# Units 30 to 67 of the weight stream: the low half of each weight tile on GpSimd instead of VectorE

## The chip, the core and the metric

One Trainium2 chip; the program runs on one of its cores. The metric is device time in microseconds (us) from the first to the last instruction of an execution, plus a small constant. It is measured over three runs; one further execution is recorded by the hardware profiler, and every row below is of that one.

## The reference, cut to what matters

One decoder layer on 512 tokens of width 2048, in float32:

- x1 = x + W_out · concat[conv_group(xn), swa_group(xn)], with xn = RMSNorm(x) and proj = xn @ W_in + b_in. The first 2048 columns of proj feed the convolution group: a GLU (a · sigmoid(gate)), a causal depthwise convolution with 31 taps over 1024 channels, LayerNorm over the channels, swish. The rest are q, k and v of a sliding-window attention with 16 heads of 64.
- y = x1 + PEER(RMSNorm(x1)): product-key retrieval of 16 of 16384 single-neuron experts for each of 8 heads. The kernel computes most tokens densely over all experts and the last tokens by gathered rows.

Matrix products have to come out at float32 precision. The kernel writes each float32 matrix as hi + lo, where hi is the value rounded to the type that TensorE multiplies fast (float32r) and lo is the rest, and sums three products: hi·hi, hi·lo and lo·hi.

## The kernel before, in words

**The weight stream.** All weights come through one stream of 628 units of 128x1024 float32 (512 KB). `stream` (lines 124 to 137) does four things for a unit: SyncE loads it into a raw buffer (line 131; two raw buffers in this part of the kernel), ScalarE rounds it into w_hi (line 135), VectorE subtracts to make w_lo (line 136), and both tiles are kept for TensorE. Of w_hi and of w_lo there are three buffers each. `unit()` asks for one unit more than is being used.

**Which units are which.** Units 0 to 51 are the input projection, thirteen groups of four units: k/v, then query groups and GLU groups in turn, and from unit 32 on only GLU groups (channels 3 to 7). Units 30 and 31 are the second half of the last query group. Units 52 to 67 are the half of the output projection that takes the attention result ("attention half", lines 572 to 590), units 68 to 83 the half that takes the convolution result ("convolution half"). Units 84 to 115 are the PEER queries, all later ones the experts.

**What lies beside the matmuls.** Two hand-made queues of small jobs are emptied a little after every unit by `pump`, by estimated costs: attention steps in the first, the convolution in the second. A GLU group ends with two multiplications from PSUM (lines 498, 499), a sigmoid, a GpSimd memset of the 30 padding columns of a new h tile (line 502; two h buffers, so it waits until the convolution of two groups before has read its h), the gated product into h (line 503), and 31 taps on VectorE (lines 287, 289), each a multiply-add of two 128x512 SBUF tiles. When all 8 channel groups are through, LayerNorm follows: their sum s (lines 455, 457), its mean by a matmul with ones (line 461, lnmu), subtraction (466), squares on ScalarE (472) summed on VectorE (473), the statistics by matmuls (262, 269), then per channel group a multiplication (480), swish (481) and the split into mh and ml (171, 172). The convolution half's first matmul needs mh, its second ml. The LayerNorm jobs are entered behind the attention half's matmuls in the program; the marks `urgent` and `high_priority` move them ahead by 200 instructions in the planner's order.

**What sets the order.** Each engine works through its own queue in a fixed order. The order comes from a planner that runs when the kernel is built: it takes, by its own estimate of the times, the instruction that is ready and stands first in the program, after priorities. The loads, w_hi and w_lo have a priority offset of 400. If an engine's real times differ from the plan, the order stays.

**GpSimd** (POOL in the profile) has, before the gathers of the PEER part begin, constants, two memsets for the v tiles and the eight memsets of h.

Of the kernel before, what the change touches and what calls it, by code (L numbers as in the profile page):

```python
# [9 lines left out]
FT = mybir.dt.float32  # L10
# [4 lines left out]
OP = mybir.AluOpType  # L15
# [12 lines left out]
START = 10  # L28
END = 250.0
PUMP = 5.4  # L30
CONV_K = 31
HD, NQ = 64, 16
NK, PH, TOPK = 128, 8, 16
# [2 lines left out]
C_N1, C_N2, C_CB, C_LG, C_LB, C_BA, C_BG, C_CW = 0, 16, 32, 40, 48, 56, 64, 72  # L36
N_PAR = C_CW + 8 * CONV_K
R_B, R_SK, R_QG, R_KG = 0, 1280, 1296, 1360
# [21 lines left out]
def hymba_layer(ctx: ExitStack, tc: tile.TileContext, xT, pos, par, row, wi, wo, wq, sk, ut, un, vt, vn,  # L60
                out_t, out_r, dbg=None):
    nc = tc.nc
# [18 lines left out]
    def later(cost, fn, *a, low=False):  # L81
        queues[low].append((cost, fn, a))
# [11 lines left out]
    def drain(low=True):  # L94
        for q in queues[:1 + low]:
            while q:
                _, fn, a = q.popleft()
                fn(*a)
# [26 lines left out]
    def stream(upto):  # L125
        while nxt[0] < min(upto, len(specs)):
            i = nxt[0]
            nxt[0] += 1
            raw = raws[-1][0].tile([128, 1024], FT, name="w_raw", bufs=raws[-1][1])
            with tc.high_priority(offset=400 if i >= 4 else 0):  # L130
                nc.sync.dma_start(raw, specs[i])
            hi = ring.tile([128, 1024], FR, name="w_hi", bufs=3)
            lo = ring.tile([128, 1024], FR, name="w_lo", bufs=3)
            with tc.high_priority(offset=400):
                nc.scalar.activation(hi, raw, AF.Copy)  # L135
                nc.vector.tensor_tensor(lo, raw, hi.bitcast(FT), op=OP.subtract)  # L136
            units[i] = (hi, lo)

    def unit(ahead=1):
        i = nxt[1]  # L140
        nxt[1] += 1
        stream(i + 1 + ahead)
        return units.pop(i)
# [19 lines left out]
    def par_col(base, c):  # L163
        return P[:, base + c:base + c + 1]
# [72 lines left out]
    for c in range(KC):  # L237
        if c % 4 == 0:
            stream(c // 4 + 1)
        xr = px.tile([128, T], FT, name="xr", bufs=4)  # L240
        nc.sync.dma_start(xr, xT[c])
        nc.scalar.activation(xh[:, c], xr, AF.Copy, scale=par_col(C_N1, c))
        nc.vector.scalar_tensor_tensor(xl[:, c], xr, par_col(C_N1, c), xh[:, c].bitcast(FT), op0=OP.mult,
                                       op1=OP.subtract)
        if c == 0:
            nc.scalar.activation(ssq, xr, AF.Square)
        else:
            sq = px.tile([128, T], FT, name="sq", bufs=2)
            nc.scalar.activation(sq, xr, AF.Square)
            nc.vector.tensor_tensor(ssq, ssq, sq, op=OP.add)  # L250
# [30 lines left out]
    def conv_chunk(c, h):  # L281
        first = [True]

        def tap(k):
            w = par_col(C_CW, c * CONV_K + k)
            if k == 0:
                nc.vector.tensor_scalar(mix_c[:, c], h[:, :T], w, par_col(C_CB, c), op0=OP.mult, op1=OP.add)
            else:
                nc.vector.scalar_tensor_tensor(mix_c[:, c], h[:, k:k + T], w, mix_c[:, c], op0=OP.mult, op1=OP.add)  # L289
        for k in range(CONV_K):  # L290
            later(0.66, tap, k, low=True)
# [192 lines left out]
    def glu_group(g):  # L484
# [15 lines left out]
        nc.scalar.activation(tg, tg, AF.Sigmoid, bias=par_col(C_BG, g))  # L500
        h = pa_.tile([128, CONV_K - 1 + T], FT, name="h", bufs=2)
        nc.gpsimd.memset(h[:, :CONV_K - 1], 0.0)
        nc.vector.scalar_tensor_tensor(h[:, CONV_K - 1:], ta, par_col(C_BA, g), tg, op0=OP.add, op1=OP.mult)
        conv_chunk(g, h)
# [279 lines left out]
    for h in range(PH):  # L784
# [6 lines left out]
        for u in range(4):  # L791
            hi, lo = unit()
# [123 lines left out]
    def step(first, us):  # L916
        tick[0] += 1
        if tick[0] > START:
            gather_until(int((tick[0] - START) * STEPS / (END - START)) + 1, first)
        pump(us)  # L920
# [18 lines left out]
    for e in range(8 * AHEAD):  # L939
# [3 lines left out]
        if e % 4 == 3:  # L943
            nc.scalar.dma_start(H[e // 4], gl)
        step(first, PUMP)
    drain()
# [149 lines left out]
```

## Time and profile before

| | us |
|---|---|
| median of 3 runs | 2863.24 (2862.2 to 2864.12) |
| the profiled execution | 2863.08 |
| its span, first to last instruction | 2861.3 |
| PE (TensorE) busy | 2811.3 (98%) |
| DVE (VectorE) busy | 2368.2 (83%) |
| ACT (ScalarE) busy | 1214.2 (42%) |
| POOL (GpSimd) busy | 471.7 (16%) |

The span is cut into 40 slices of 71.5 us for the overview of the page; a digit is the busy share of a slice in tenths. The third to the seventh slice hold the stretch of units 30 to 67. Busy times of neighbouring instructions overlap a little: VectorE's 128x1024 subtraction is listed at 1.23 us, and the next one starts 1.14 us after it. TensorE's busy time is modelled from pipelined matmuls, and a full share does not say that it runs at its best clock; the granted clock stands in a column of its own (1.00 is 2.4 GHz).

### The profile page before, as it was taken

To read this page: it belongs to the slowest core of one execution; us is meant where nothing else is said; L and a number is where in the kernel's file an instruction comes from. 1 tells how busy PE (TensorE), PEld (TensorE's weight loads), DVE (VectorE), ACT (ScalarE), POOL (GpSimd) and SP (SyncE) were. 2 spreads that over 40 slices of the span, in tenths; PEclk is the share of its full clock that TensorE was granted. 3 is DMA by queue.
4 is the path that set the end of the run, shared out by engine and by line. 5 is a ranking of instruction groups with operands and counts; after the bars stand their busy time and mean duration, and the time that the engine had idled before them with its cause. 6 is when DMAs were issued, how large, how long until landed. Compare 5 with 4: busy or idle time off the path is not lost. (4 is left out here: it accounts for less than half of the span.)

```text
span 2861.3 us, 43542 instructions
## 1 busy us (share of the span) xinstructions
PE 2811.3 (98%) x16995; PEld 2688.8 (94%) x16995; DVE 2368.2 (83%) x3586; ACT 1214.2 (42%) x1879; POOL 471.7 (16%) x337
## 2 busy tenths in 40 slices
PE   8999999999999999999999999999999999999999
PEld 8998877788899999999999999999999999999999
DVE  7888996569999887777787878878888899997984
ACT  5666434343343787666332333333333333333332
POOL 0000000000002222212212222222222223222320
PEclk9999999999999999999999999999999999999999
DMA  5222332523249999899998989898898999998994
GB/s 174 75 67 74 115 100 85 170 93 136 89 157 345 325 325 339 311 341 339 349 351 321 343 313 359 335 336 336 326 344 323 372 361 350 354 366 329 358 347 147
DMA packets 204207, 764.00 MB, mean 267 GB/s; under 512 B 18593, under 2 KB 70945, under 8 KB 160417
## 3 DMA queue, kind: packets, MB, share of 16 engines
q1 hardware_dynamic: 103584, 378.66, 36.7%
q0 software_dynamic: 46080, 335.56, 31.0%
q10 hardware_dynamic: 54336, 47.00, 5.0%
q8 instruction: 133, 2.18, 0.3%
q14 instruction: 74, 0.60, 0.1%
HBM read 716.42 MB, written 44.70 MB: 266 GB/s over the span
## 5 line engine op out<-in xcount | busy, mean ns | idle before, releaser
L135 ACT ACTIVATE w_hi<-w_raw 128x1024 fp32r<-128x1024 f32 x628 | 666.0, 1061 | 1277.7 <-PE mm L981 536.1
L136 DVE TENSOR_TENSOR w_lo<-w_raw,w_hi 128x1024 fp32r<-128x1024 f32 x628 | 772.1, 1233 | 276.6 <-ACT w_hi L135 275.4
L932 PE MATMUL mm<-nl,w_hi 128*128 128x352 f32 x2048 | 668.2, 326 | 0.0
L930 PE MATMUL mm<-nh,w_hi 128*128 128x352 f32 x2048 | 664.9, 325 | 1.0 <-ACT w_hi L135 1.0
L979 PE MATMUL mm<-ah,w_hi 128*128 128x352 f32 x2048 | 658.4, 323 | 7.4 <-DVE acc L989 7.4
L933 PE MATMUL mm<-nh,w_lo 128*128 128x352 f32 x2048 | 664.0, 325 | 0.0
L981 PE MATMUL mm<-al,w_hi 128*128 128x352 f32 x2048 | 660.3, 323 | 0.0
L982 PE MATMUL mm<-ah,w_lo 128*128 128x352 f32 x2048 | 645.0, 323 | 12.7 <-DVE w_lo L136 12.5
L982 PEld LDWEIGHTS mm<-ah,w_lo 128*128 128x128 f32 x2048 | 380.9, 188 | 18.0 <-DVE w_lo L136 17.9
L979 PEld LDWEIGHTS mm<-ah,w_hi 128*128 128x128 f32 x2048 | 384.0, 188 | 9.2 <-DVE acc L989 7.6
L930 PEld LDWEIGHTS mm<-nh,w_hi 128*128 128x128 f32 x2048 | 385.3, 188 | 1.5 <-ACT w_hi L135 1.3
L933 PEld LDWEIGHTS mm<-nh,w_lo 128*128 128x128 f32 x2048 | 385.4, 188 | 0.1
L932 PEld LDWEIGHTS mm<-nl,w_hi 128*128 128x128 f32 x2048 | 384.8, 188 | 0.1
L981 PEld LDWEIGHTS mm<-al,w_hi 128*128 128x128 f32 x2048 | 384.8, 188 | 0.0
L826 POOL DMA_INDIRECT grow<-un,idx x86 | 121.3, 1411 | 898.9 <-DVE grow L842 591.3
L859 DVE SCALAR_TENSOR_TENSOR yrow<-grow,h,yrow 128x2048 f32<-128x2048 f32 x107 | 251.4, 2349 | 1.5 <-DMA grow<-vn,idxb 1.4
L842 DVE SCALAR_TENSOR_TENSOR grow<-grow,xrow 128x2048 f32<-128x2048 f32 x107 | 244.6, 2286 | 0.8 <-DMA grow<-un,idxb 0.8
L989 DVE TENSOR_TENSOR acc<-acc,mm 128x352 f32<-128x352 f32 x240 | 118.8, 521 | 87.4 <-PE mm L982 87.3
L826 POOL DMA_INDIRECT grow<-vn,idx x85 | 125.4, 1475 | 391.5 <-DVE yrow L859 381.6
L289 DVE SCALAR_TENSOR_TENSOR mix_c<-h,par,mix_c 128x512 f32<-128x512 f32 x240 | 173.8, 750 | 1.6
L859 DVE SCALAR_TENSOR_TENSOR yrow<-xrow,h,yrow 128x2048 f32<-128x2048 f32 x53 | 124.6, 2351 | 0.0
L842 DVE SCALAR_TENSOR_TENSOR yrow<-yrow,xrow 128x2048 f32<-128x2048 f32 x53 | 121.2, 2286 | 2.9 <-DMA xrow<-XB 2.9
(274 smaller groups left out, 3979.3 us busy)
## 6 DMA issues: line engine op xcount, KB each, us to landing
w_raw<-ut SPq DMA_DIRECT2D x256, 512.0 KB
w_raw<-vt SPq DMA_DIRECT2D x256, 512.0 KB
w_raw<-wi SPq DMA_DIRECT2D x52, 512.0 KB
G<-gt ACTq DMA_DIRECT2D x22, 1024.0 KB
Gb<-G SPq DMA_DIRECT2D x16, 1408.0 KB
w_raw<-wo SPq DMA_DIRECT2D x32, 512.0 KB
w_raw<-wq SPq DMA_DIRECT2D x32, 512.0 KB
H<-gl ACTq DMA_DIRECT2D x18, 704.0 KB
```

Source lines behind the costliest of these rows:

```text
L135: nc.scalar.activation(hi, raw, AF.Copy)
L136: nc.vector.tensor_tensor(lo, raw, hi.bitcast(FT), op=OP.subtract)
L289: nc.vector.scalar_tensor_tensor(mix_c[:, c], h[:, k:k + T], w, mix_c[:, c], op0=OP.mult, op1=OP.add)
L826: i = nc.gpsimd.indirect_dma_start(out=g, out_offset=None, in_=src, in_offset=bass.IndirectOffsetOnAxis(ap=at, axis=0))
L842: nc.vector.scalar_tensor_tensor(g, g, 1.0, rows["x"], op0=OP.mult, op1=OP.mult, accum_out=h3[:, k:k + 1])
L859: nc.vector.scalar_tensor_tensor(y, g, h3[:, k:k + 1], y, op0=OP.mult, op1=OP.add)
L930: m = nc.tensor.matmul(bank, hi[:, s], nh[:, k, :TD], start=k == 0, stop=False)
L932: nc.tensor.matmul(bank, hi[:, s], nl[:, k, :TD], start=False, stop=False)
L933: nc.tensor.matmul(bank, lo[:, s], nh[:, k, :TD], start=False, stop=k == KC - 1)
L979: m = nc.tensor.matmul(banks[j], hi[:, ws], ah[:, ee], start=ee == 0, stop=False)
L981: nc.tensor.matmul(banks[j], hi[:, ws], al[:, ee], start=False, stop=False)
L982: nc.tensor.matmul(banks[j], lo[:, ws], ah[:, ee], start=False, stop=ee == 7)
```

## The change

`stream` picks the engine of the subtraction by the unit's number: GpSimd for units 30 to 67, VectorE for all others. The loads, w_hi, buffers, priorities and the order of the program's text stay.

```diff
+POOL_LO = (30, 68)
...
             with tc.high_priority(offset=400):
                 nc.scalar.activation(hi, raw, AF.Copy)
-                nc.vector.tensor_tensor(lo, raw, hi.bitcast(FT), op=OP.subtract)
+                eng = nc.gpsimd if POOL_LO[0] <= i < POOL_LO[1] else nc.vector
+                eng.tensor_tensor(lo, raw, hi.bitcast(FT), op=OP.subtract)
             units[i] = (hi, lo)
```

## Rows read from the trace of the kernel before

**Rows 1.** The page's overview: busy tenths in 40 slices.
```profile
PE   8999999999999999999999999999999999999999
DVE  7888996569999887777787878878888899997984
POOL 0000000000002222212212222222222223222320
```

**Rows 2.** Busy by stretch: window, length; PE, PEld, DVE, ACT, POOL busy; clock, DMA.
```profile
203.00:437.00 234.00, 231.46 (x1202) 195.43 (x1201) 217.37 (x388) 107.89 (x208) 0.50 (x4) 1.00 0.28 93
```

**Rows 3.** VectorE's groups in 203 to 437 us: count | busy us, mean ns | idle before.
```profile
L289 DVE SCALAR_TENSOR_TENSOR mix_c<-h,par,mix_c 128x512 f32<-128x512 f32 x180 | 129.0, 751 | 1.0
L136 DVE TENSOR_TENSOR w_lo<-w_raw,w_hi 128x1024 fp32r<-128x1024 f32 x37 | 45.3, 1225 | 6.3 <-ACT w_hi L135 6.1
L172 DVE TENSOR_TENSOR pl<-ptr,ph 128x512 fp32r<-128x512 f32 x14 | 9.6, 687 | 2.6 <-ACT ph L171 2.6
L398 DVE CUSTOM_DVE_ANT_0 sm<-sc,maskb 128x256 f32<-128x256 f32 x24 | 9.1, 423 | 0.0
...
L498 DVE TENSOR_TENSOR tg<-mm,rstd 128x512 f32<-128x512 f32 x6 | 4.1, 686 | 0.0
```

**Rows 4.** VectorE in order of time, 436 to 467 us: start, length, instruction [idle before].
```profile
436.69 0.68 DVE L457 TENSOR_TENSOR s<-s,mix_c 128x512 f32<-128x512 f32 x1
...
444.05 4.91 DVE L466 TENSOR_TENSOR mix_c<-mix_c,mu 128x512 f32<-128x512 f32 x8 [1.72 <-ACT mu L463]
...
454.25 3.08 DVE L473 TENSOR_TENSOR lnss<-lnss,lnsq 128x512 f32<-128x512 f32 x4
...
462.29 4.87 DVE L480 TENSOR_TENSOR mix_c<-mix_c,stat 128x512 f32<-128x512 f32 x8 [1.25 <-PE stat L269]
```

**Rows 5.** TensorE in order of time, 442 to 466 us.
```profile
442.36 1.02 PE L461 MATMUL lnmu<-s,ones 128*128 128x512 f32 x2
...
457.39 0.40 PE L582 MATMUL mm<-mah,w_lo 128*128 128x512 f32 x1
...
465.10 2.08 PE L580 MATMUL mm<-mh,w_hi 128*128 128x512 f32 x4 [2.86 <-ACT mh L171]
```

**Rows 6.** Busy by stretch behind the attention half, columns as in rows 2.
```profile
460.00:470.00 10.00, 5.42 (x17) 3.93 (x18) 6.86 (x12) 9.30 (x16) 0.00 (x0) 0.61 0.18 54
470.00:480.00 10.00, 10.00 (x39) 7.98 (x39) 4.42 (x6) 4.00 (x7) 0.00 (x0) 0.87 0.00 0
```

**Rows 7.** GpSimd's memsets of large tiles, grouped as in rows 3.
```profile
L855 POOL MEMSET yrow<- 128x2048 f32 x1 | 1.8, 1812 | 10.9 <-DMA out_r<-yrow 10.9
L348 POOL MEMSET vh<- 128x1024 f32 x1 | 1.0, 954 | 40.0 <-PE rowstat L262 40.0
```

**Rows 8.** One GpSimd instruction: duration ns min/median/max.
```profile
L826 POOL DMA_INDIRECT grow<-un,idx x86: 935/1681/2751, 678.0 to 1662.3; - x86
```

**Rows 9.** GpSimd and VectorE in order of time around 928 and 946 us.
```profile
927.88 0.94 POOL L826 DMA_INDIRECT grow<-un,idx  x1 [5.18 <-DVE grow L842]
...
946.33 1.68 POOL L826 DMA_INDIRECT grow<-un,idx  x1 [5.75 <-DVE grow L842]
...
928.73 1.23 DVE L136 TENSOR_TENSOR w_lo<-w_raw,w_hi 128x1024 fp32r<-128x1024 f32 x1 [1.11 <-ACT w_hi L135]
...
945.98 1.22 DVE L136 TENSOR_TENSOR w_lo<-w_raw,w_hi 128x1024 fp32r<-128x1024 f32 x1
```

**Rows 10.** ScalarE's w_hi two units apart, in order of time.
```profile
428.86 1.06 ACT L135 ACTIVATE w_hi<-w_raw 128x1024 fp32r<-128x1024 f32 x1 [4.01 <-PE mm L581]
...
440.01 1.06 ACT L135 ACTIVATE w_hi<-w_raw 128x1024 fp32r<-128x1024 f32 x1 [4.01 <-PE mm L581]
```

**Rows 11.** Who waited for the loads of line 131, 200 to 460 us (us, times).
```profile
  ACT w_hi L135: 1.4, 1
```

**Rows 12.** GpSimd's queue in order of time, 246 to 387 us.
```profile
309.99 0.12 POOL L502 MEMSET h<- 128x30 f32 x1 [63.27 <-DVE mix_c L289]
...
386.60 0.12 POOL L502 MEMSET h<- 128x30 f32 x1 [32.45 <-DVE mix_c L289]
```

## The prediction, made before the result was known

> **What bounds the kernel now.** I read the page's overview first. TensorE's row shows 9 in every slice but the first; VectorE's shows 8 and 9 up to the sixth, and GpSimd's shows 0 until the gathers start [rows 1]. So TensorE bounds the kernel, and a change on other engines can give back only time in which TensorE waits, or add to it. The next view is busy time by stretch: between 203 and 437 us, where units 30 to 66 get their low halves, VectorE is busy 217.4 of 234 us, GpSimd 0.5, ScalarE 107.9, and TensorE is short of the window by 2.5 us [rows 2]. There is little to win inside the stretch.
>
> The loss lies at its end. In TensorE's order of time the attention half's last matmul starts at 457.39 and the convolution half's first at 465.10, after a wait for ScalarE's mh [rows 5]. A matmul of this shape follows the last one after 0.23 us (two units of 24 in 11.15 us [rows 10]), so TensorE lacks 465.10 - 457.62 = 7.5 us. The clock pays again: 0.61 in the ten microseconds of the gap and 0.87 in the next ten, against 1.00 before [rows 6]. From 465.1 to 480 that costs roughly 10 x 0.13 = 1.3 us behind 470 and 5 x 0.5 = 2.4 us ahead of it (half speed while the gap is fresh), 3.7 us in all. The transition is worth 11 us.
>
> What ends last there is LayerNorm. In VectorE's order, the sum s is complete at 436.69 + 0.68 = 437.4; the mean's matmul lnmu runs at 442.36, the subtractions start at 444.05, the last squares are summed by 457.3, the multiplications start at 462.29 [rows 4, 5]. From lnmu to the first mh matmul it is 465.10 - 442.36 = 22.7 us. So the question is when s is complete, and that is VectorE's work: s comes after the last of the taps.
>
> **What the change removes.** 38 subtractions leave VectorE, 37 of them by 437 us: 45.3 us busy [rows 3], or 37 x 1.14 = 42 us of its time, by the spacing of starts. Their input and everything else stays: no instruction more or fewer.
>
> **What it adds.** 37 subtractions on GpSimd up to 437 us, and one behind it. The trace has no arithmetic instruction on GpSimd. The nearest rows are its memsets: 0.954 us for 1024 elements per partition and 1.812 for 2048 [rows 7], so 0.86 us for each stream of 1024 and 0.1 to start. The subtraction reads two such streams and writes one. All three at once gives 0.95 us, the lower end; two reads one after the other with the write beside give 1.8; all in turn give 2.7, the upper end. The row is the same engine and shape but only writes; I take the middle of the last two, 2.3 us.
>
> The Trainium skill ("GPSIMD Engine Reference", section "Elementwise — side-by-side cycle accounting") gives 4497 ns for such an operation on 2048 elements; half of it, 2.25 us, is an estimate from that page, and no run here shows it yet. With it the sum below would end 2 us lower.
>
> **Whether GpSimd works beside VectorE or in turn with it** is the disputed price. Nearly all that VectorE does in the stretch are operations with two inputs from SBUF: 129.0 us of taps beside the subtractions [rows 3]. Below, the price can be nothing: GpSimd runs beside them, and VectorE is 42 us ahead. Above, each waits for the other for the whole instruction: 37 x 2.3 = 85 us are taken from VectorE where 42 were given. The only GpSimd instruction in the trace that runs beside VectorE in numbers is the indirect DMA; the same instruction takes 0.94 to 2.75 us, median 1.68 [rows 8]. Around 928 us, with VectorE idle for 1.11 us, it took 0.94; around 946 us, between two-input operations without a gap, 1.68 [rows 9]. That is one pair and no proof, but it is nearest to the upper end: GpSimd is held up while VectorE is busy. I take turns as the case.
>
> The Trainium skill ("SBUF — State Buffer", section "Who interferes with whom") speaks against this change: it says that a VectorE instruction with two SBUF inputs contends with a GpSimd instruction that reads SBUF, and that the second to issue is fully blocked until the first is done. The rows just named do not contradict it.
>
> **The sum.** Demand on VectorE up to 437 us: 85 - 42 = 43 us more. Cover: its idle time of 234 - 217 = 17 us, and the operations that read from PSUM, which can run beside GpSimd: pl 9.6, scores 9.1, the evacuations of line 498 4.1 and as much for 499, 27 us, of which the share in which GpSimd is active (85 of 234) gives 10 [rows 2, 3]. 43 - 27 = 16 us remain, so s is complete at about 453.4. Of that, 5.0 us are free, since lnmu today stands 442.36 - 437.4 behind its input. 0.3 is left for a start. The chain behind it keeps its 22.7 us, which puts the first mh matmul at 453.7 + 22.7 = 476.4 instead of 465.10: 11.3 us later. Wherever the planner puts lnmu in TensorE's order, this end is the same: a place before 453 makes TensorE wait there instead of at the end of the half. The price of the clock is paid already and stays. Profiled execution: 2863.1 + 11.3 = 2874.4. The median is 0.16 us above that execution, so the forecast is 2874.5. Each 0.1 us of GpSimd's duration moves it by up to 3.7; between 2.1 and 2.6 us it runs from 2867 to 2886.
>
> **What hides the rest.** A low half that comes 1 to 2 us later is covered by the ring: w_hi, which is made two units ahead, itself waits for TensorE to free a buffer, 4.01 us in both rows, and two units are 11.2 us [rows 10]. Raw buffers come free as much later; waits for loads were 1.4 us in 260 [rows 11]. Without this cover each unit would cost up to 1 us, 38 in all. On GpSimd's queue the subtractions stand between the memsets of h, which waited for the taps, 63.27 us at 309.99 and at last 32.45 at 386.60 [rows 12]; what is queued behind such a memset is priced as a rival. Work after 465 us only shifts: GpSimd's gathers begin at 678 [rows 8].
>
> **The rivals.**
> *Beside each other.* GpSimd and VectorE do not hold each other up. VectorE is up to 42 us ahead, s is there long before TensorE takes it, and lnmu moves to the earliest place its priority allows: it is entered some 50 instructions (38 taps, 8 sums, evacuations) behind the last matmul, the mark moves it by 200, and a unit has about 35, so it can come 4 units of 5.6 us before the end of the half, at 435.4. That is 7 us earlier; mh comes at 458.1, the gap of 7.5 shrinks to 0.6, the clock stays up (3.7), and perhaps 1 us of waits on ml remains: -9.6, or 2853.5. For it: VectorE's own rows show no sign of a GpSimd instruction. Against it: rows 8 and 9. It decides as long as a low half costs VectorE less than the 1.14 us it gave.
> *A draw.* Turns, but short ones (1.4 to 1.9 us) or half of them: s stays within 5 us of 437.4, which the wait of lnmu takes up: 2858 to 2868, in the middle 2863. For it: the lower rows of the bound. It is also what comes if the planner fills VectorE in another way.
> *GpSimd's queue.* The order is planned, so a memset of h can stand before a low half; with VectorE 16 us late, the memset waits as long, the ring covers 11.2, and TensorE stalls about 5 us at each of three or four memsets in the stretch. With the sum above: 2874 + 15 to 20 = 2891. For it: GpSimd's longest waits are these. Against it: low halves have the high priority.
>
> **How the numbers follow.** Turns as summed 0.38, beside each other 0.32, a draw 0.19, GpSimd's queue 0.11. A measurement tells 0.2%, 5.7 us, from no change. Faster: 0.30 of the second and 0.02 of the draw, 0.32. Slower: 0.36 + 0.11 + 0.03, 0.50. The rest, 0.18, within. The likeliest one's own range is 2867 to 2886; since cases of both signs hold the chance, the range goes from 2852, just below the second case, to 2890.
>
> **What would show it.** Right: taps of 0.75 us lengthen to 2 or 3 beside a GpSimd subtraction of 2.1 to 2.6 us; s is complete after 448, the first mh matmul comes after 470. Wrong: the taps keep 0.75 us; s is complete before 435 and the gap before the convolution half is under 3 us. If GpSimd's queue is the place, TensorE waits for w_lo between 246 and 390 us behind a memset.

## The result, and the profile after

| | before | after |
|---|---|---|
| median, us | 2862.72 (4 runs) | 2881.53 (2877.32 to 2883.91, 4 runs) |
| ratio | | 1.0066 (95% interval 1.0054 to 1.0079) |
| profiled execution; its span, us | 2863.08; 2861.3 | 2880.95; 2879.1 |

The change costs 18.8 us, 0.66%. The forecast was 11.3 us slower, 2874.5, with a range from 2852 to 2890.

The overview of the page after, in 40 slices, answers to [rows 1]; GpSimd now shows work in the fourth to the seventh slice, and TensorE its first 7 in the sixth:
```profile
PE   8999979999999999999999999999999999999999
DVE  7888997659999888788678878888888899897994
POOL 0003332000002222222211222212222232322330
PEclk9999989999999999999999999999999999999999
```

Busy time by stretch of the changed kernel; the first row answers to [rows 2] and has its columns (window, length; PE, PEld, DVE, ACT, POOL busy; granted clock; DMA), the others cut the stretch and what follows into parts:
```profile
203.00:437.00 234.00, 209.91 (x1077) 174.70 (x1077) 219.60 (x334) 98.12 (x196) 82.37 (x36) 0.95 0.25 81
...
203.00:246.00 43.00, 40.83 (x307) 38.54 (x307) 40.53 (x92) 26.22 (x68) 13.05 (x6) 1.00 0.19 60
246.00:310.00 64.00, 62.48 (x323) 51.49 (x322) 53.40 (x106) 36.21 (x79) 20.64 (x8) 1.00 0.21 68
310.00:364.00 54.00, 50.52 (x223) 40.70 (x223) 52.74 (x57) 15.63 (x25) 21.24 (x10) 0.97 0.34 117
364.00:437.00 73.00, 56.08 (x228) 43.97 (x227) 72.93 (x82) 20.06 (x27) 27.45 (x12) 0.86 0.25 79
```
Read the third and the first column together. VectorE no longer has the 37 subtractions that it had in this window [rows 3], and is busier than before, 219.6 us against 217.4, with 54 instructions fewer done. TensorE lacks 24.1 us where it lacked 2.5: 7 in the first three parts and 17 in the last, where its clock is down as well. What VectorE spends its time on, in the groups of the same view (203 to 473 us, so that all 180 taps and all 38 units are in):
```profile
L291 DVE SCALAR_TENSOR_TENSOR mix_c<-h,par,mix_c 128x512 f32<-128x512 f32 x180 | 182.0, 1040 | 2.1
L174 DVE TENSOR_TENSOR pl<-ptr,ph 128x512 fp32r<-128x512 f32 x14 | 9.3, 679 | 0.0
L400 DVE CUSTOM_DVE_ANT_0 sm<-sc,maskb 128x256 f32<-128x256 f32 x24 | 9.1, 417 | 0.0
...
L289 DVE TENSOR_SCALAR mix_c<-h,par 128x512 f32<-128x512 f32 x6 | 5.3, 885 | 0.2
...
L413 DVE TENSOR_TENSOR mx<-mx 128x4 f32<-128x4 f32 x8 | 4.4, 550 | 1.3 <-ACT sm L411 1.3
...
L500 DVE TENSOR_TENSOR tg<-mm,rstd 128x512 f32<-128x512 f32 x5 | 3.4, 684 | 0.0
```
The 180 taps take 182.0 us instead of 129.0 [rows 3]. The operations that read one input from PSUM (pl, the scores of L400, tg) kept their durations within 0.01 us. And GpSimd's new group, with its mean of 2.61 us:
```profile
L138 POOL TENSOR_TENSOR w_lo<-w_raw,w_hi 128x1024 fp32r<-128x1024 f32 x38 | 98.9, 2606 | 165.2 <-ACT w_hi L136 149.8 <-DVE mx L406 7.2 <-PE mm L496 5.9
```

How one holds up the other is seen by putting GpSimd's and VectorE's order of time of the changed kernel side by side. GpSimd:
```profile
300.97 2.39 POOL L138 TENSOR_TENSOR w_lo<-w_raw,w_hi 128x1024 fp32r<-128x1024 f32 x1 [12.43 <-ACT w_hi L136]
...
338.04 2.58 POOL L138 TENSOR_TENSOR w_lo<-w_raw,w_hi 128x1024 fp32r<-128x1024 f32 x1 [3.73 <-ACT w_hi L136]
...
389.87 0.12 POOL L504 MEMSET h<- 128x30 f32 x1 [13.20 <-DVE mix_c L291]
389.99 2.69 POOL L138 TENSOR_TENSOR w_lo<-w_raw,w_hi 128x1024 fp32r<-128x1024 f32 x1
```
and VectorE:
```profile
301.64 1.74 DVE L413 TENSOR_TENSOR mx<-mx 128x4 f32<-128x4 f32 x1
...
338.28 2.89 DVE L291 SCALAR_TENSOR_TENSOR mix_c<-h,par,mix_c 128x512 f32<-128x512 f32 x1
...
372.36 18.11 DVE L291 SCALAR_TENSOR_TENSOR mix_c<-h,par,mix_c 128x512 f32<-128x512 f32 x24
390.39 0.68 DVE L501 TENSOR_TENSOR ta<-mm,rstd 128x512 f32<-128x512 f32 x1
390.99 2.23 DVE L291 SCALAR_TENSOR_TENSOR mix_c<-h,par,mix_c 128x512 f32<-128x512 f32 x1
```
An operation on 128x4 elements, 0.16 us elsewhere, takes 1.74 us and ends at 303.38, where GpSimd's ends (303.36). The tap at 338.28 takes 2.89 us: it ends 0.55 us behind GpSimd's end at 340.62. The evacuation at 390.39, which has one input in PSUM, lies inside GpSimd's third subtraction (389.99 to 392.68) and keeps its 0.68 us; the tap behind it takes 2.23.

Where TensorE pays, in its own order of time at the start of the attention half (answers to [rows 5]):
```profile
375.50 0.40 PE L496 MATMUL mm<-xh,w_lo 128*128 128x512 f32 x1
377.44 0.73 PE L582 MATMUL mm<-mah,w_hi 128*128 128x512 f32 x2 [1.54 <-ACT mah L173]
391.12 0.80 PE L582 MATMUL mm<-mah,w_hi 128*128 128x512 f32 x1 [12.95 <-DVE ta L501]
393.88 0.80 PE L582 MATMUL mm<-mah,w_hi 128*128 128x512 f32 x1 [1.96 <-DVE tg L500]
...
458.26 1.12 PE L463 MATMUL lnmu<-s,ones 128*128 128x512 f32 x2 [0.77 <-DVE s L459]
...
488.72 0.40 PE L584 MATMUL mm<-mah,w_lo 128*128 128x512 f32 x1
488.96 0.62 PE L582 MATMUL mm<-mh,w_hi 128*128 128x512 f32 x2
```
The last GLU group's matmuls end at 376, so ta could run then. In VectorE's fixed order 24 taps from 372.36 stand ahead of it, so it starts at 390.39, and TensorE waits 13 us for the bank. While TensorE stands still, and in most of the ten microseconds behind that, the granted clock is at half, 1.2 GHz:
```profile
380.00:390.00 10.00, 0.00 (x0) 0.00 (x0) 10.00 (x16) 1.03 (x2) 0.13 (x2) 0.50 0.00 0
390.00:400.00 10.00, 6.45 (x16) 4.44 (x17) 10.00 (x15) 0.72 (x1) 2.67 (x1) 0.56 0.17 54
```
At the other end of the half, the gap of 7.5 us [rows 5] is gone: the convolution half's first matmul starts 0.24 us behind the attention half's last. It starts 23.9 us later than before (488.96 against 465.10). Three terms make that up. The attention half starts 11.4 us late (377.44 against 366.05): in the attention steps up to 364 us TensorE waits 7 us for VectorE, 4.5 of them for pl, and before the change it waited for nothing there. The half itself takes 19.9 us longer (111.5 against 91.6), with the 13 us for ta, smaller waits and the slow clock. The gap of 7.5 us is saved. Without the slow clock that stood behind that gap before, the convolution half's last mh matmul is 20.8 us later (578.8 against 558.0), and the program's last matmuls 17.8 (2871.0 against 2853.2). The 3 us between come back in smaller waits behind 600 us and were not pursued.

### The profile page after: what moved, and what is told of

Its sections match the earlier page's. It is cut to its first block, busy times and chain, and to the rows that moved or that the text cites. A ratio compares the mean times of both kernels' runs of the same rounds, so it can differ in the third digit from the quotient of the medians.

```text
span 2879.1 us, 43545 instructions
## 1 busy us (share of the span) xinstructions
PE 2817.2 (98%) x16995; PEld 2690.9 (93%) x16995; DVE 2394.2 (83%) x3548; ACT 1210.8 (42%) x1879; POOL 567.4 (20%) x375
## 5 line engine op out<-in xcount | busy, mean ns | idle before, releaser
L138 DVE TENSOR_TENSOR w_lo<-w_raw,w_hi 128x1024 fp32r<-128x1024 f32 x590 | 719.5, 1224 | 273.0 <-ACT w_hi L136 270.4
L291 DVE SCALAR_TENSOR_TENSOR mix_c<-h,par,mix_c 128x512 f32<-128x512 f32 x240 | 226.8, 966 | 2.7
L138 POOL TENSOR_TENSOR w_lo<-w_raw,w_hi 128x1024 fp32r<-128x1024 f32 x38 | 98.9, 2606 | 165.2 <-ACT w_hi L136 149.8
```

Of the source, the lines that this page charges most:

```text
L138: eng.tensor_tensor(lo, raw, hi.bitcast(FT), op=OP.subtract)
```

## The experiments

Theory 1: a GpSimd instruction that reads SBUF and a VectorE operation with two inputs from SBUF take turns; VectorE falls behind, and TensorE pays at whatever VectorE owes it next. The rivals are the planner's new order alone (2), any GpSimd instruction (3), GpSimd's queue (4), the place of ta alone (5).

**The relief without the price.**
```diff
-            lo = ring.tile([128, 1024], FR, name="w_lo", bufs=3)
+            moved = POOL_LO[0] <= i < POOL_LO[1]
+            lo = hi if moved else ring.tile([128, 1024], FR, name="w_lo", bufs=3)
...
-                eng = nc.gpsimd if POOL_LO[0] <= i < POOL_LO[1] else nc.vector
-                eng.tensor_tensor(lo, raw, hi.bitcast(FT), op=OP.subtract)
+                if not moved:
+                    nc.vector.tensor_tensor(lo, raw, hi.bitcast(FT), op=OP.subtract)
```


> For units 30 to 67 no low half is computed at all (the third product uses w_hi again), so VectorE is relieved of 38 subtractions and GpSimd gets nothing. Theory 1 (GpSimd's reads and VectorE's two-input operations take turns; the relief itself is good): no stall in front of the attention half, s complete before 435 us, 5 to 10 us faster than before, 2853 to 2858. Theory 2 (the planner's new order, with the subtractions gone from VectorE's queue, is what puts the evacuations late; contention does not matter): TensorE waits for ta here as well, 10 us or more, and the time is 2870 or above.

2848.44 us, ratio 0.9951 (0.9934 to 0.9968): 11.7 us faster where 5 to 10 were expected, and 4.6 us below the expected time. There is no wait for ta; s is complete at 409.7, the mean's matmul runs at 428.4 instead of 442.4 and the first mh matmul at 458.9, with no gap:
```profile
428.40 1.02 PE L464 MATMUL lnmu<-s,ones 128*128 128x512 f32 x2
458.94 0.62 PE L583 MATMUL mm<-mh,w_hi 128*128 128x512 f32 x2
```
Theory 2 is out. VectorE's load in this stretch is worth what the rival "beside each other" had put on it (9.6) and a little more.

**A GpSimd instruction that only writes.**
```diff
-                eng = nc.gpsimd if POOL_LO[0] <= i < POOL_LO[1] else nc.vector
-                eng.tensor_tensor(lo, raw, hi.bitcast(FT), op=OP.subtract)
+                if POOL_LO[0] <= i < POOL_LO[1]:
+                    nc.gpsimd.memset(lo.bitcast(FT), 0.0)
+                else:
+                    nc.vector.tensor_tensor(lo, raw, hi.bitcast(FT), op=OP.subtract)
```


> For units 30 to 67 GpSimd only fills the low half with zeros (one write stream, no input from SBUF) and VectorE computes none; lo is left out of the sum for these units. Theory 1 (the turns come from reading SBUF): a 128x4 or 128x512 operation of VectorE is nowhere lengthened to GpSimd's end, taps keep 0.75 us, 2853 to 2860. Theory 3 (any GpSimd instruction beside VectorE holds it up, write or read): taps of up to 1.6 us beside the memsets of 0.95 us, the time between the two, 2860 to 2868. Theory 4 (GpSimd's queue: the low halves stand behind memsets of h that wait for taps): TensorE waits for w_lo here too, several us each time.

2850.15 us, 0.9958 (0.9941 to 0.9975), like the run before and 3 us below the expected 2853 to 2860. GpSimd's group and the taps (the second fence: all 240, duration min/median/max in ns):
```profile
L138 POOL MEMSET w_lo<- 128x1024 f32 x38 | 36.4, 957 | 204.8 <-PE mm L498 97.8 <-PE mm L586 62.9 <-DVE ta L503 16.0
```
```profile
L293 DVE SCALAR_TENSOR_TENSOR mix_c<-h,par,mix_c x240: 659/748/755, 88.4 to 407.4; 128x512 f32<-128x512 f32 x120
```
38 memsets of 0.957 us beside the taps lengthen none of them. Theories 3 and 4 are out: these instructions stood in the same queue among the same memsets of h, and TensorE waited for no w_lo, nor did it in the changed kernel.

This run settles the order too. Between the first of the six ta and the last one, VectorE has the same work here, in the run before and in the changed kernel: 132 taps and 152 other operations (in the kernel before 115 taps, 24 subtractions and the same 152). The taps of that stretch, in the changed kernel and here:
```profile
L291 DVE SCALAR_TENSOR_TENSOR mix_c<-h,par,mix_c 128x512 f32<-128x512 f32 x132 | 125.4, 977 | 1.5
L293 DVE SCALAR_TENSOR_TENSOR mix_c<-h,par,mix_c 128x512 f32<-128x512 f32 x132 | 95.0, 748 | 1.5
```
With the same work ahead of it, the last ta starts at 390.39 there and at 363.54 here, where it waits for TensorE and not the other way round. So the order alone did not make ta late; the longer operations did.

**One stream read.**
```diff
-                eng = nc.gpsimd if POOL_LO[0] <= i < POOL_LO[1] else nc.vector
-                eng.tensor_tensor(lo, raw, hi.bitcast(FT), op=OP.subtract)
+                if POOL_LO[0] <= i < POOL_LO[1]:
+                    nc.gpsimd.tensor_copy(lo, raw)
+                else:
+                    nc.vector.tensor_tensor(lo, raw, hi.bitcast(FT), op=OP.subtract)
```


> For units 30 to 67 GpSimd copies the raw tile into the low half's place: one stream read from SBUF and one written; the low half itself is left out (lo holds the raw weights). Theory 1 in the form that any read from SBUF takes turns with VectorE's second input: taps are lengthened to GpSimd's end, up to about 1.8 us, VectorE loses 38 x (1.0 to 1.3) against 38 x 1.14 given back, so about the time of before, 2855 to 2868. If one read stream goes beside VectorE as the memset does: no tap above 0.80 us and 2846 to 2852.

2850.78 us, 0.9964 (0.9952 to 0.9975). The taps are lengthened as expected, and the time, 2855 to 2868, was missed:
```profile
L138 POOL CAST w_lo<-w_raw 128x1024 fp32r<-128x1024 f32 x38 | 50.5, 1328 | 193.5 <-PE mm L498 88.2 <-PE mm L586 60.6 <-DVE ta L503 16.0
```
```profile
L293 DVE SCALAR_TENSOR_TENSOR mix_c<-h,par,mix_c x240: 662/749/1619, 88.5 to 414.2; 128x512 f32<-128x512 f32 x120
```
Taps reach 1.62 us, so a single read stream takes turns too. But the copies take 1.33 us in the mean, not 2.61 (1.18 without one of 6.91 us), and the 180 taps of the stretch 144.5 us instead of 129.2 in the first run: 15 us taken, 42 given back.

**The price without the relief.**
```diff
+POOL_LO = (30, 52)
...
                 nc.vector.tensor_tensor(lo, raw, hi.bitcast(FT), op=OP.subtract)
+                if POOL_LO[0] <= i < POOL_LO[1]:
+                    spare = ap_.tile([128, 1024], FT, name="spare", bufs=1)
+                    nc.gpsimd.tensor_tensor(spare, raw, hi.bitcast(FT), op=OP.subtract)
```


> VectorE keeps all its subtractions, and for units 30 to 51 GpSimd computes the same difference once more into a spare tile that nobody reads: no relief, the turns alone. Theory 1: VectorE loses up to 22 x 2.6 = 57 us to GpSimd beside a full load, and TensorE waits in the input projection or in front of the attention half; slower than the run with units 30 to 51 moved by up to the 22 x 1.14 = 25 us that VectorE was relieved of there: 2890 to 2910. If GpSimd cost VectorE nothing: within 0.2% of before.

2894.15 us, 1.0118 (1.0094 to 1.0142): 32 us for 22 instructions of GpSimd whose result nobody reads. They take 3.10 us each here, beside a VectorE that is busy 169.4 of the 173 us from 203 to 376 (158.6 in the changed kernel):
```profile
L140 POOL TENSOR_TENSOR spare<-w_raw,w_hi 128x1024 f32<-128x1024 f32 x22 | 68.1, 3096 | 114.7 <-ACT w_hi L136 106.9 <-issue 6.7 <-POOL spare L140 0.9
```
TensorE's waits are spread: 13.2 us for pl in the attention steps, 6.5 for mah. The edit has a second effect, that GpSimd reads the raw buffer too; but between 350 and 400 us the loads waited 48.9 us for VectorE's late subtractions to free one and 2.3 us for GpSimd. The next run, which moves the same 22, costs 19.4 us over its own kernel before, 13 less.

**Each part of the range alone**, `POOL_LO = (30, 52)`:

> GpSimd has units 30 to 51 only (the input projection), 22 of the 38; VectorE has those of the attention half again. Theory 1: about the same wait for ta in front of the attention half, since that lateness is collected in 203 to 376 us, and then a LayerNorm chain with less cover lost: 2868 to 2880. If the loss were collected in the attention half, within 0.2% of before.

2879.59 us, 1.0062 (1.0045 to 1.0079): the 22 units of the input projection alone cost as much as all 38. The time is as expected, the place is not: TensorE waits only 2.0 us for ta, and 7.5 for mah:
```profile
383.33 1.22 PE L582 MATMUL mm<-mah,w_hi 128*128 128x512 f32 x2 [7.50 <-ACT mah L173]
```
ScalarE makes mah (382.66) behind a w_hi that waited 8.4 us for its load, and the raw buffer for that load was free only when VectorE's subtraction, late behind 11 taps, had read the buffer (376.90). So here VectorE owed TensorE a raw buffer first. `POOL_LO = (52, 68)`:

> GpSimd has units 52 to 67 only (the attention half), 16 of the 38. Theory 1: 16 x 2.6 = 42 us of GpSimd against 16 x 1.14 = 18 given back, so s comes up to 20 us later than at 437; no wait for ta in front of the attention half, but the gap ahead of the convolution half grows from 7.5 to 15 to 25 us: 2868 to 2880. If only lateness from the input projection matters, within 0.2% of before.

2874.39 us, 1.0048 (1.0030 to 1.0067). Here the wait stands at the mean's matmul in TensorE's order of time, one of the two places that the forecast allowed, and s is about 10 us late:
```profile
447.80 2.08 PE L463 MATMUL lnmu<-s,ones 128*128 128x512 f32 x2 [12.52 <-DVE s L459]
479.99 0.62 PE L582 MATMUL mm<-mh,w_hi 128*128 128x512 f32 x2
```
The expectation had put it at the gap ahead of the convolution half, which is gone, and had no wait for ta; there was one of 3.5 us. The two parts do not add up (19.4 and 12.3 us against 18.8 for both); the likely reason, not tested by itself, is that VectorE catches up while TensorE waits. `POOL_LO = (68, 84)`:

> GpSimd has units 68 to 83 (the convolution half), where VectorE is busy half of the time and the taps are done. Theory 1: the turns cost something only in the LayerNorm chain around 449 to 475 us, where VectorE's multiplications and splits stand in front of the first matmuls: 0 to 4 us slower, the same otherwise. If GpSimd's own 2.6 us were what TensorE waits for, waits for w_lo would appear here too, one per unit.

2860.99 us, 0.9997 (0.9984 to 1.0010), no change, as expected. VectorE is held up here as well: 14 additions x<-x,xr, which took 9.0 us in the kernel before, take 22.2, the longest 2.90:
```profile
L558 DVE TENSOR_TENSOR x<-x,xr 128x512 f32<-128x512 f32 x14 | 22.2, 1630 | 0.0
```
But in the kernel before VectorE is busy only 54 of the 95 us from 465 on, and TensorE does not wait for what comes late. GpSimd's 2.54 us each are no price in themselves, and neither are the turns where VectorE has time to spare.

**The place of ta**, first by priority:
```diff
-        nc.vector.tensor_tensor(tg, banks[1], rstd, op=OP.mult)
-        nc.vector.tensor_tensor(ta, banks[0], rstd, op=OP.mult)
+        with tc.high_priority(offset=400):
+            nc.vector.tensor_tensor(tg, banks[1], rstd, op=OP.mult)
+            nc.vector.tensor_tensor(ta, banks[0], rstd, op=OP.mult)
```


> The changed kernel, with the two PSUM evacuations of a GLU group (ta, tg) given the low halves' priority, so that they stand ahead of the taps in VectorE's order. Theory 1 with the lateness only moved (VectorE owes about 40 us to GpSimd wherever the evacuations stand): the wait of 13 us for ta goes, s comes as late or later, the gap ahead of the convolution half comes back; 2872 to 2882. Theory 5 (the wrong place of ta in VectorE's order is the whole loss): the 13 us and the slow clock behind them go and nothing comes back; 2855 to 2866.

2883.40 us, 1.0080 (1.0063 to 1.0096), but it tells nothing: ta stayed behind the same 24 taps (wait 12.5 us). The planner places an instruction when it thinks it is ready, and by its times VectorE has presumably done those taps by then. So the banks were freed without VectorE:
```diff
-        nc.vector.tensor_tensor(tg, banks[1], rstd, op=OP.mult)
-        nc.vector.tensor_tensor(ta, banks[0], rstd, op=OP.mult)
+        nc.scalar.activation(tg, banks[1], AF.Copy)
+        nc.scalar.activation(ta, banks[0], AF.Copy)
+        nc.vector.tensor_tensor(tg, tg, rstd, op=OP.mult)
+        nc.vector.tensor_tensor(ta, ta, rstd, op=OP.mult)
```


> The changed kernel, with a GLU group's two PSUM banks copied out by ScalarE first (two copies of about 0.6 us per group), the two multiplications following on VectorE from SBUF: the banks come free without VectorE. Theory 1 (VectorE owes its time wherever the wait stands): the wait of 13 us for ta in front of the attention half goes, and a wait of 8 us or more appears at s or at mal; 2868 to 2882. Theory 5 (the late evacuation is the whole loss): nothing comes back, 2852 to 2866.

2881.29 us, 1.0076 (1.0051 to 1.0101). TensorE's order of time shows the wait moved to the next thing VectorE owes, the low half of the attention result:
```profile
377.76 2.08 PE L584 MATMUL mm<-mah,w_hi 128*128 128x512 f32 x4 [2.99 <-ACT mah L173]
395.01 0.80 PE L585 MATMUL mm<-mal,w_hi 128*128 128x512 f32 x1 [15.17 <-DVE mal L174]
```
Theory 5 is out; as theory 1 expected, ta was only the first thing owed, and s is complete at 458.2 as in the changed kernel. (The two multiplications now have both inputs in SBUF and can be held up themselves; the longest took 2.38 us.) The control, the same edit in the kernel before:

> The control: the kernel before with the same evacuation by ScalarE. VectorE has the same number of operations and no GpSimd beside it, and no bank was waited for: within 0.2% of before by both theories.

2865.70 us, 1.0016 (1.0004 to 1.0029), no gain, 3 us more; so the edit did not hide a gain in the run above.

**A small relief that doesn't read beside VectorE.**
```diff
-                nc.vector.tensor_scalar(mix_c[:, c], h[:, :T], w, par_col(C_CB, c), op0=OP.mult, op1=OP.add)
+                nc.scalar.activation(mix_c[:, c], h[:, :T], AF.Identity, scale=w, bias=par_col(C_CB, c))
```


> The kernel before, with the first of the 31 taps of each channel group (a multiply-add with one tensor input, 0.46 us of VectorE) on ScalarE. By theory 1 VectorE's relief alone is what counts: 6 such taps lie between 203 and 437 us, 2.8 us, so s is up to 2.8 us earlier and the time 0 to 3 us shorter, 2859 to 2863, hardly above the noise. Rival: ScalarE's queue makes the tap late and VectorE waits for it, 0 to 5 us longer.

2860.69 us, 0.9995 (0.9982 to 1.0008): not told apart from no change. No kernel here that does the whole work is measurably faster than the one before.

## Why the prediction was right, and where its sum was not

**Turns.** Right, and the side that decided. The forecast had GpSimd at 2.3 us per unit and VectorE losing 85 - 27 = 58 us, 68% of GpSimd's 85. Measured: 2.61 us; and up to the end of s, where GpSimd has been busy 92 us, VectorE's operations together are about 62 us longer than before, 67% (53.0 on the taps, 3.1 on L413, 2.0 on L289, the rest on other small ones). The duration was sized 12% too low, the cover a little too low too. The rule of the Trainium skill on two SBUF inputs ("SBUF — State Buffer", section "Who interferes with whom") agrees with these rows: 1.74 us on 128x4 elements, ended by GpSimd's end. The estimate of 2.25 us from the Trainium skill ("GPSIMD Engine Reference", section "Elementwise — side-by-side cycle accounting") is 5% below the shortest in the changed kernel, 2.37 (2.34 in the run with units 68 to 83).

**s.** Forecast complete at 453.4, measured at 458.2 (457.52 + 0.69); "after 448" held. The working holds too: 62 us lost less the 42 given back make 20, and s came 20.8 us later than before, where the forecast had 16.

**The path behind it.** This step failed: "Wherever the planner puts lnmu in TensorE's order, this end is the same", the first mh matmul 22.7 us behind s, at 476.4. It came 30.7 us behind s, at 488.96, and not because of LayerNorm: the attention half itself ended at 488.9. Two things were wrong in that step.

First, the place of lnmu is not indifferent, because the half's matmuls that stand behind lnmu run only when its wait is over. In the kernel before, 15.0 us lay between lnmu and the half's last matmul (442.36 to 457.39 [rows 5]), less than LayerNorm's 22.7. In the changed kernel the planner put lnmu earlier, with 30.5 us of the half behind it (458.26 to 488.72); in the run without low halves it is the same distance, 428.40 to 458.94 for the first mh matmul. So with s at 458.2 the first mh matmul could not come before about 488.7, whatever TensorE had waited for ahead of that. Units 52 to 67 alone show it where the wait is at lnmu: 12.5 us of wait, and the first mh matmul 32.2 us behind lnmu, at 479.99, where 22.7 would have given 470.5. That the time of this run (2874.4) is the forecast's is luck: the forecast was for all 38 units, and here s is only 10 us late instead of 16 while the path behind it is 9.5 us longer.

Second, the forecast let VectorE's lateness meet TensorE at one place, s. VectorE owes TensorE something before that: pl in the attention steps, the bank of the last GLU group, raw buffers, and mal, and all of them stand behind taps in an order fixed beforehand. TensorE waited there, 7 us in the attention steps and 17 up to 437 us, and behind the long wait the clock was at half until about 400 us. These waits and the one for s overlap: TensorE reached lnmu at 457.3, just before s, and waited 0.8 us for it. The gap at the end of the half went, and the clock's price moved with the wait instead of staying where it was (1.00 behind the attention half now, 0.50 and 0.56 at its start).

**The cover.** For the low halves the ring held: no wait of TensorE for w_lo in the changed kernel between 190 and 600 us, and at most 1.1 us in any other run. For the loads it held less well: ScalarE's w_hi waited 7.1 us for loads between 200 and 460 us, against 1.4 before [rows 11], because raw buffers came free late. The rival with GpSimd's queue did not happen; memsets of h with low halves behind them did occur (at 353.77 and 389.87, the second after 13.2 us of GpSimd's time), without a wait of TensorE for w_lo. At the second TensorE stood waiting for ta anyway.

**Beside each other.** Its price was right: the run with the relief alone gave 11.7 us where 9.6 were put on it. Its condition, a low half under 1.14 us of VectorE, was missed: up to 476 us VectorE's operations are about 66 us longer than before, 66 / 38 = 1.7 us per low half.

**A reading.** VectorE's first slice in [rows 1] is 7, not 8; nothing hangs on it.

## What to carry to other kernels

Before an elementwise operation goes to an idle GpSimd, look at what VectorE does at that time: if it is full of operations with two inputs from SBUF, an instruction of GpSimd that reads two streams there took more from VectorE here than it gave back (1.7 us for 1.14), a copy with one stream took less (0.4), and a write-only memset took nothing. With a fixed order on each engine, lateness is paid from the first thing on that the late engine owes the bounding one, not only at the end of the chain that was late before; list all of them in order of time. Behind each, add up the bounding engine's own work that stands behind the wait: if that is longer than the chain, it sets the end. An engine's load can be priced by leaving the work out: it showed in one run that 11.7 us were to be had from VectorE, and that the rest was the price of the way chosen.

## What the runs showed of the hardware

One-input operations of VectorE from SBUF are not all free of this: the first tap, a multiply-add of one tensor with two scalars (L289), took 2.60 us at 369.83 beside GpSimd's pair at 366.78, 0.53 to 0.55 elsewhere:
```profile
366.78 5.37 POOL L138 TENSOR_TENSOR w_lo<-w_raw,w_hi 128x1024 fp32r<-128x1024 f32 x2 [7.35 <-ACT w_hi L136]
369.83 2.60 DVE L289 TENSOR_SCALAR mix_c<-h,par 128x512 f32<-128x512 f32 x1
```
A copy with one read stream of 1024 elements took 1.04 us on GpSimd at the least, 1.33 in the mean, and cost VectorE 0.4 us each (15.3 / 38), less than its duration; the subtraction with two streams took 2.34 at the least. One copy took 6.91 us, from 358.80, while VectorE's taps beside it ran on at 0.67 us each (11 taps in 7.37 us from 357.44), so it seems that GpSimd can be the one that waits, through several operations; this is one record and was not pursued.
